# A two-layer attention and expert kernel: double-width products in every second u block, a joint pair choice, and another order of the v blocks

## The chip, the cores and the metric

The kernel runs on one core of a Trainium2 chip. The metric is device time in microseconds (us), from several executions of one program. TensorE (PE) does the matrix products and loads their stationary operand (PEld). VectorE (DVE), ScalarE (ACT) and GpSimd (POOL) work on tiles in on-chip memory, and SyncE (SP) starts most transfers. Each engine works through its own queue in order and waits on semaphores.

## The reference, cut to what matters

Two layers, each an attention mixer and an expert layer with residuals, on 256 tokens of width 1024. The change lies in the expert layer and in the step from layer 0's expert layer to layer 1's mixer (`fox`).

```python
def peer_ffn(x, w_q, sub_keys, u, v):        # 8 heads, 128x128 experts, 16 picked per head
    q = (x @ w_q).reshape(B, S, 8, 2, 128)
    s_half = jnp.einsum('bshpc,hpkc->bshpk', q, sub_keys)
    top_s, top_i = lax.top_k(s_half, 16)
    cand_s = top_s[..., 0, :, None] + top_s[..., 1, None, :]
    cand_i = top_i[..., 0, :, None] * 128 + top_i[..., 1, None, :]
    best_s, best_pos = lax.top_k(cand_s.reshape(B, S, 8, 256), 16)
    experts = jnp.take_along_axis(cand_i.reshape(...), best_pos, axis=-1)
    gate = jax.nn.softmax(best_s, axis=-1)
    h = jax.nn.gelu(einsum(u[experts], x))
    return einsum(gate * h, v[experts])
```

## The kernel before, in words

The kernel does not gather experts. For all 16384 experts, in 128 blocks of 128, it forms the products with u, applies gelu, multiplies by a gate that is zero where an expert is not picked, and multiplies by v. fp32 operands are kept as two parts, `hi` (rounded) and `lo` (the rest), and a product is three matrix products.

**The u sweep** is the loop over `b in range(NB)`, NB = 128, in `peer`. `load_split` (L727 and after) loads one block (512 KB) into `raw`, ACT casts it to `hi` (L116) and DVE subtracts to give `lo` (L117); each of the three tags has three buffers. `feat_block` runs, for each of 8 chunks, three products of 256 columns: hi with `xh` (L744), hi with `xl` (L747), lo with `xh` (L748). The result lies in a PSUM tile of the tag "h", which has two buffers. `values` applies gelu on ACT (L981, L984), and on DVE multiplies the tokens whose gates are already there (L985).

Beside it runs a list of small steps, `steps()`: the rest of `top_keys`; then `best_pairs`, which chooses 16 of 50 candidate pairs for each head and token and turns positions into expert numbers with masks (L881 to L930); then 32 `gate_steps` of 8 tokens, each with four DVE products of 1024 elements (L952 to L956), 16 TensorE products (L963, L964), and multiplications or copies into the gate store (L970, L972). Each step yields an estimated price, and after block b steps are taken until 1.66 us times b+1 are spent. This sets only the order in which instructions are written; a list scheduler then orders each engine's queue by its own cost model, with the written order as priority, and moves a later instruction forward where buffers and data allow. `pin` keeps an instruction in its written place.

**The gate store**: blocks 0 to 63 lie in `gte`, which takes the tile tagged "E" (one buffer); blocks 64 to 127 lie in `arena`, 256 columns each. The residual `h` lies in `arena` columns 10240 to 12287, the place of blocks 104 to 111, and waits in DRAM meanwhile (`h_out`, `h_in`).

**The v sweep** takes blocks 64 to 127, then `h_in`, then 0 to 63. `v_gate` splits the gates of two blocks (128x512), `v_whole` loads and splits a block of v with `load_split`, and 12 products of 512 columns accumulate in four PSUM tiles (L1020 to L1022). The last two blocks are held back for `fin(tt, nh)`, which finishes one accumulator and adds it to `h` (L1050).

**The step to layer 1**: after `fin`, `nxt.piece` transposes `h` (L150) for the next norm. `fox` takes the tile "E" anew as `HL`; `w_half` loads half of a weight tile into `arena` and splits it into `HL`. The first two halves are split with the subtraction on POOL (`(GP, GP)`), the next two with it on DVE.

Of the kernel before, what the change touches and what calls it, by code (L numbers as in the profile page):

```python
# [14 lines left out]
ALU = mybir.AluOpType  # L15
# [24 lines left out]
def body(ctx, tc, A, out):  # L40
# [4 lines left out]

    const = ctx.enter_context(tc.tile_pool(name="const", bufs=1))
    arena = const.tile([P, LC], F32, name="arena")
    xh = const.tile([P, 8, S], F32R, name="xh")
    xl = const.tile([P, 8, S], F32R, name="xl")
    cst = const.tile([P, 160], F32, name="cst")  # L50
    ident = cst[:, :P]
    gcols = cst[:, P:].rearrange("p (i c) -> p i c", i=4)
# [64 lines left out]
        (eng or V).tensor_tensor(lo, raw, hi.bitcast(F32), ALU.subtract)  # L117

    def squares(ss, tt, nh, junk):
        ACT.activation(ar(junk + nh * 512, 512), h[:, tt, nh * 512:nh * 512 + 512], AF.Square, accum_out=ss[:, nh:nh + 1])  # L120

    def rstd_of(ss, tt):

# [134 lines left out]
    def nsa():  # L258
# [329 lines left out]
        h_in(xsrc)  # L588
        return out_proj(HL, A["w_out0"], oh, ol, 1, [marks[i] for i in (2, 5, 7)]), marks[7]

    def fox(norm):
        HL = tl(big, "E", [16384], F32R, 1)
        oh = view(HL[:, 12288:14336], (8, S))
        ol = view(HL[:, 14336:16384], (8, S))
        qa = ar(6144, 16, S)
        ka = ar(10240, 16, S)
        vt = ar(14336, 2, D)
        wsrc = [A["w_in1"][:, off * 8:(off + n) * 8].rearrange("p (c n) -> p c n", c=8) for off, n in FOX_TILES]

        ws = [w_half(HL, wsrc[4][:, i * 4:i * 4 + 4], 512, (GP, GP)) for i in range(2)]  # L600
        for nh in range(2):
            steps = [lambda: norm.piece(1, 0), lambda: norm.piece(1, 1)]
            o = proj_tok(HL, wsrc[4 + nh], 512, xh, xl, ws=None if nh else ws, steps=steps)
# [147 lines left out]
    def peer(li, norm, mark):  # L751
# [97 lines left out]
        off += 512  # L849
        msk = [ar(off + i * 1024, 1024).bitcast(F16).rearrange("p (h j k) -> p h j k", h=8, j=16) for i in range(2)]  # L850
        off += 2048
        assert off <= LC - 2048, off

        hkT = tl(vst, "hkT", [4, S], F16, 1)
        def picked(m, x, dst):

            for q in range(2):
                hs = slice(4 * q, 4 * q + 4)
                V.tensor_tensor(m[:, hs], m[:, hs], x[:, hs].unsqueeze(3).broadcast_to((P, 4, 16, 16)), ALU.mult)
                yield 1.2  # L860
            for n in (8, 4, 2):
                V.tensor_tensor(m[:, :, :n], m[:, :, :n], m[:, :, n:2 * n], ALU.add)
            V.tensor_tensor(dst, m[:, :, 0], m[:, :, 1], ALU.add)
            yield 1.6

        def best_pairs():

            for tt in range(2):
                V.tensor_copy(idxh[:, tt], idx[:, tt].rearrange("p (h u) k -> p h u k", u=2))
                V.tensor_copy(dl[:, tt, :, 0:1], idxh[:, tt, :, 0, 0:1])  # L870
                V.tensor_tensor(dl[:, tt, :, 1:16], idxh[:, tt, :, 0, 1:16], idxh[:, tt, :, 0, 0:15], ALU.subtract)
                o_ = 0
                for a in range(9):
                    n = CAND_N[a] if a < 8 else 8
                    if a < 8:
                        i0 = top[:, tt, :, 1, 0:n]
                        i1 = top[:, tt, :, 0, a:a + 1].broadcast_to((P, 8, n))
                    else:
                        i0 = top[:, tt, :, 0, 8:16]
                        i1 = top[:, tt, :, 1, 0:1].broadcast_to((P, 8, n))  # L880
                    V.tensor_tensor(cand[:, tt, :, o_:o_ + n], i0, i1, ALU.add)  # L881
                    o_ += n
                    if a in (2, 8):
                        yield 1.0
                for hh in range(8):
                    c1 = cand[:, tt, hh]
                    c2 = cand2[:, hh % 2]
                    V.max(best[:, tt, hh, 0:8], c1)
                    V.max_index(pos[:, tt, hh, 0:8], best[:, tt, hh, 0:8], c1)
                    V.match_replace(c2, best[:, tt, hh, 0:8], c1, FMIN)  # L890
                    V.max(best[:, tt, hh, 8:16], c2)
                    V.max_index(pos[:, tt, hh, 8:16], best[:, tt, hh, 8:16], c2)
                    yield 1.25
                V.tensor_tensor(gf[:, tt], best[:, tt], best[:, tt, :, 0:1].broadcast_to((P, 8, 16)), ALU.subtract)

                V.tensor_copy(posh[:, tt], pos[:, tt])
                for hh in range(8):
                    V.tensor_tensor(msk[0][:, hh], posh[:, tt, hh].unsqueeze(1).broadcast_to((P, 16, 16)), st3, ALU.is_ge)
                    if hh % 4 == 3:
                        yield 1.3  # L900
                yield from picked(msk[0], dl[:, tt], i12[:, tt, 0])

                V.tensor_scalar(bh[:, tt], posh[:, tt], -42.0, 0.0, ALU.add, ALU.max)
                V.tensor_tensor(bh[:, tt], posh[:, tt], bh[:, tt], ALU.subtract)
                for i, (st, ln) in enumerate(((16, 16), (24, 8), (29, 5), (33, 4), (36, 3), (38, 2), (40, 2), (42, 2))):
                    V.tensor_scalar(th[:, tt], posh[:, tt], float(st), float(ln), ALU.is_ge, ALU.mult)
                    V.tensor_tensor(bh[:, tt], bh[:, tt], th[:, tt], ALU.subtract)
                    if i % 4 == 3:
                        yield 1.7
                for hh in range(8):  # L910
                    V.tensor_tensor(msk[1][:, hh], bh[:, tt, hh].unsqueeze(1).broadcast_to((P, 16, 16)), jt3, ALU.is_equal)
                    if hh % 4 == 3:
                        yield 1.15
                yield from picked(msk[1], idxh[:, tt, :, 1, :], i12[:, tt, 1])
                g3 = gf[:, tt]
                pin(ACT.activation(g3, g3, AF.Exp))
                gs = smt("gs", [8])
                V.tensor_reduce(gs, g3, AX.X, ALU.add)
                V.reciprocal(gs, gs)
                V.tensor_scalar(gs, gs, GSC, None, ALU.mult)  # L920
                V.tensor_tensor(g3, g3, gs.unsqueeze(2).broadcast_to((P, 8, 16)), ALU.mult)
                yield 4.2
# [8 lines left out]
                yield 0.3  # L931

# [11 lines left out]
        def gate_steps():  # L944


            for t0 in range(0, S, 8):
# [25 lines left out]
                    done[1] += 4  # L973
                yield 1.2

        def values(b, o):
            n = done[1]
            (x, _, _), = slots(b, b + 1, slice(0, S))
            x = x[:, 0]
            if n < S:  # L980
                ACT.activation(x[:, n:], o[:, n:S], AF.Gelu_apprx_tanh)  # L981
            if n > 0:
                gt = t2k(S)
                ACT.activation(gt[:, :n], o[:, :n], AF.Gelu_apprx_tanh)  # L984
                V.tensor_tensor(x[:, :n], gt[:, :n], x[:, :n], ALU.mult)  # L985
            done[0] = b + 1
# [5 lines left out]

        aux, spent = steps(), 0.0
        for b in range(NB):
            values(b, feat_block(load_split(uT[b])))
            if b < 2:
                scores(14 + b, qTs[14 + b])
            while spent < 1.66 * (b + 1):
                spent += next(aux, 1e9)

        acc = [[pst("m", bufs=4) for _ in range(2)] for _ in range(2)]
# [26 lines left out]
                for tt in range(2):  # L1028
                    v_mm(tt, nh, gg, vv[nh], first)

        for b in range(NE, NB):
            v_block(b, b == NE)
        h_in()
        if li == 1:
            gain = t4k(D)
            SP.dma_start(gain, A["final_norm"].broadcast_to((P, D)))
        for b in range(NE - 2):
            v_block(b)

        tail = []  # L1040
        for b in range(NE - 2, NE):
            gg = v_gate(b)
            tail.append((gg, v_whole(b)))

        def fin(tt, nh):
            for i, (gg, vv) in enumerate(tail):
                v_mm(tt, nh, gg, vv[nh], last=i == 1)
            for q in range(2):
                hs = slice(nh * 512 + q * 256, nh * 512 + q * 256 + 256)
                V.tensor_tensor(h[:, tt, hs], acc[tt][nh][:, q * 256:q * 256 + 256], h[:, tt, hs], ALU.add)  # L1050

        if li == 0:
            nxt = Norm(2, xh, xl, 6144)
            fin(0, 0)
            fin(0, 1)
            fin(1, 0)
            nxt.piece(0, 0)
            fin(1, 1)
            nxt.piece(0, 1)
# [97 lines left out]
```

## Time and profile before

| | |
|---|---|
| runs shown | 1953.0, 1954.05, 1956.66 us (median 1954.05) |
| the profiled execution | 1953.7 us, of which the span of its records is 1951.9 us |
| busy share of the span | PE 98%, PEld 88%, DVE 72%, ACT 51%, POOL 6% |
| layer 0 by time | mixer and query products to 242 us, u sweep to about 650 us, v sweep and `fin` to 1004 us |
| layer 1 by time | mixer from 1004 us, u sweep to about 1595 us, v sweep to 1943.7 us, end 1951.9 us |

Busy PE time counts each product from its start to its modelled end, and successive products overlap, so the pace of a stretch is read from start to start of the products.

### The profile page before, as it was taken

Reading aid. Unit: us, or ns where it says so; the run is one execution under the profiler, and the core shown is the slowest. Engines: PE = TensorE matmul, PEld = TensorE weight load, DVE = VectorE, ACT = ScalarE, POOL = GpSimd, SP = SyncE. Lnnn points to the kernel's source line nnn. Section 1 sums busy time; section 2 is a strip of 40 time slices with the busy share of each in tenths; the row PEclk is TensorE's granted clock in tenths of the full one; section 3 lists DMA queues with packets and bytes.
Section 4 is the critical chain, followed back from the end, with each engine's and each line's share of the span. In section 5 each row is a group of like instructions: output and inputs, shape, how many; then the busy total and the mean of one; then the engine's idle time right before and its main releaser. Section 6 shows DMA issues by size and latency. Waiting matters only on the chain.

```text
span 1951.9 us, 34088 instructions
## 1 busy us (share of the span) xinstructions
PE 1913.0 (98%) x13131; PEld 1718.6 (88%) x13131; DVE 1411.2 (72%) x3006; ACT 994.0 (51%) x1886; POOL 120.5 (6%) x80
## 2 busy tenths in 40 slices
PE   8889999999999999999999999999999999999998
PEld 6767999999999888888879799999999998888886
DVE  8687999478888655555586799956788975555555
ACT  5475645554444444444464655445544444444444
POOL 2001700000000000000040061000000000000001
PEclk9989999999999999999999999999999999999999
DMA  6623555554555666666654245565555556666664
GB/s 231 226 76 120 161 164 185 184 160 155 162 154 160 212 232 214 195 193 192 194 191 172 71 154 160 174 192 164 158 157 161 153 174 194 193 215 205 194 194 140
DMA packets 90194, 340.92 MB, mean 175 GB/s; under 512 B 9872, under 2 KB 12336, under 8 KB 84656
## 3 DMA queue, kind: packets, MB, share of 16 engines
q1 hardware_dynamic: 89744, 338.22, 54.6%
q8 instruction: 103, 1.69, 0.4%
q10 hardware_dynamic: 288, 0.52, 0.1%
q14 instruction: 59, 0.48, 0.1%
HBM read 334.48 MB, written 4.19 MB: 174 GB/s over the span
## 4 chain that ended last, share of the span: by engine, by line
PE 76%; DVE 15%; ACT 4%; issue 2%; DMA 1%; POOL 0%; SPq 0%; ACTq 0%; DVEq 0%
PE m L1021 12%; PE m L1022 12%; PE m L1020 12%; PE h L747 8%; PE h L744 8%; PE h L748 8%; DVE lo L117 5%; ACT hi L116 3%; PE m L963 2%; PE m L200 2%; PE m L202 2%; PE m L201 2%; PE m L964 1%; DVE vhl L956 1%; DVE vraw L955 1%
## 5 line engine op out<-in xcount | busy, mean ns | idle before, releaser
L117 DVE TENSOR_TENSOR lo<-raw,hi 128x1024 fp32r<-128x1024 f32 x516 | 634.9, 1231 | 397.9 <-ACT hi L116 394.3
L116 ACT CAST hi<-raw 128x1024 fp32r<-128x1024 f32 (+1 forms) x572 | 576.6, 1010 | 637.8 <-PE m L1022 294.7
L748 PE MATMUL h<-xh,lo 128*128 128x256 f32 x2048 | 581.5, 284 | 2.3 <-DVE lo L117 2.2
L744 PE MATMUL h<-xh,hi 128*128 128x256 f32 x2048 | 580.4, 283 | 1.4 <-ACT E L981 1.3
L747 PE MATMUL h<-xl,hi 128*128 128x256 f32 x2048 | 580.4, 283 | 0.0
L1021 PE MATMUL m<-lo,vhl 128*128 128x512 f32 x1024 | 399.0, 390 | 0.1
L1020 PE MATMUL m<-hi,vhl 128*128 128x512 f32 x1024 | 399.0, 390 | 0.0
L1022 PE MATMUL m<-hi,vhl 128*128 128x512 f32 x1024 | 398.8, 389 | 0.0
L748 PEld LDWEIGHTS h<-xh,lo 128*128 128x128 f32 x2048 | 386.6, 189 | 4.8 <-DVE lo L117 4.0
L744 PEld LDWEIGHTS h<-xh,hi 128*128 128x128 f32 x2048 | 386.4, 189 | 2.3 <-ACT E L981 2.0
L747 PEld LDWEIGHTS h<-xl,hi 128*128 128x128 f32 x2048 | 386.6, 189 | 0.0
L1021 PEld LDWEIGHTS m<-lo,vhl 128*128 128x128 f32 x1024 | 192.5, 188 | 40.4 <-DVE lo L117 0.5
L1020 PEld LDWEIGHTS m<-hi,vhl 128*128 128x128 f32 x1024 | 192.5, 188 | 40.1
L1022 PEld LDWEIGHTS m<-hi,vhl 128*128 128x128 f32 x1024 | 192.5, 188 | 39.7
L117 POOL TENSOR_TENSOR lo<-raw,hi 128x512 fp32r<-128x512 f32 x56 | 79.4, 1438 | 242.4 <-ACT hi L116 242.3
L972 ACT ACTIVATE arena<-m 128x256 f32<-128x256 f32 (+25 forms) x128 | 37.6, 303 | 79.9 <-DVE arena L970 75.9
L117 DVE TENSOR_TENSOR E<-arena,E 128x1024 fp32r<-128x1024 f32 (+2 forms) x60 | 70.8, 1208 | 10.1 <-ACT E L116 9.7
L744 PE MATMUL h<-E,hi 128*128 128x256 f32 x240 | 70.3, 293 | 3.0 <-ACT arena L817 3.0
L116 ACT CAST E<-arena 128x1024 fp32r<-128x1024 f32 (+2 forms) x68 | 62.2, 956 | 17.8 <-PE m L660 9.7
L117 DVE TENSOR_TENSOR vhl<-E,vhl 128x512 fp32r<-128x512 f32 x64 | 44.1, 688 | 34.1 <-ACT vhl L116 34.1
L748 PE MATMUL h<-E,lo 128*128 128x256 f32 x240 | 68.1, 284 | 0.0
L963 PE MATMUL m<-vhl 128*128 128x128 f16 x512 | 65.4, 218 | 2.7 <-DVE vhl L956 0.2
(300 smaller groups left out, 2476.9 us busy)
## 6 DMA issues: line engine op xcount, KB each, us to landing
raw<-in_u SPq DMA_DIRECT2D x256, 512.0 KB, 3.5
raw<-in_v SPq DMA_DIRECT2D x256, 512.0 KB, 4.2
arena<-in_w_in SPq DMA_DIRECT2D x18, 1024.0 KB, 5.2
raw<-in_wq SPq DMA_DIRECT2D x32, 512.0 KB, 3.7
arena<-in_w SPq DMA_DIRECT2D x8, 1024.0 KB, 5.3
arena<-in_w_out SPq DMA_DIRECT2D x8, 1024.0 KB, 5.1
hd<-arena SPq DMA_DIRECT2D x3, 1024.0 KB, 5.7
arena<-hd SPq DMA_DIRECT2D x3, 1024.0 KB, 5.9
```

The lines of the kernel that those rows point to most:

```text
L116: ACT.copy(hi, raw)
L117: (eng or V).tensor_tensor(lo, raw, hi.bitcast(F32), ALU.subtract)
L200: PE.matmul(o[:, :n], sh[:, cc, tsl], wh[:, c], start=cc == 0, stop=False)
L201: PE.matmul(o[:, :n], sh[:, cc, tsl], wl[:, c], start=False, stop=False)
L202: PE.matmul(o[:, :n], sl[:, cc, tsl], wh[:, c], start=False, stop=cc == 7)
L744: t = PE.matmul(o[:, :S], hi[:, c % 4], sh[:, c], start=c == 0, stop=False)
L747: PE.matmul(o[:, :S], hi[:, c % 4], sl[:, c], start=False, stop=False)
L748: PE.matmul(o[:, :S], lo[:, c % 4], sh[:, c], start=False, stop=c == 7)
L963: PE.matmul(o, o2[:, k, :, u], oh[:, k, :, u], start=True, stop=False)
L1020: PE.matmul(acc[tt][nh], gh[:, ts], vh, start=first, stop=False)
L1021: PE.matmul(acc[tt][nh], gh[:, ts], vl, start=False, stop=False)
L1022: PE.matmul(acc[tt][nh], gl[:, ts], vh, start=False, stop=last)
```

## The change

Four things. First, `xh` and `xl` become the two halves of one tile `x2`, so that `wide_block` can multiply `hi` with both in one product of 512 columns; odd u blocks use it: 8 products of 512 and 8 of 256 columns in place of 24 of 256. The two halves of the result are then added, with a copy on ACT and an addition on DVE. Second, `best_pairs` does both token halves in one instruction where it can, and `picked` writes its mask in one instruction and uses doubled tables (`d2`, `s2nd`); the budget falls from 1.66 to 1.5. Third, v goes 96 to 111, 0 to 63, 64 to 95, 112 to 127, `h_in` follows the first 16 blocks, three blocks are held back, and the norm's squares go to a small ring (`t2k`). Fourth, `fox_early` takes "E" in the last part of layer 0's v sweep and loads and splits `fox`'s first weights in eight pieces between v blocks, on ACT and DVE.

```diff
-    xh = const.tile([P, 8, S], F32R, name="xh")
-    xl = const.tile([P, 8, S], F32R, name="xl")
+    x2 = const.tile([P, 8, 2, S], F32R, name="x2")
+    xh, xl = x2[:, :, 0], x2[:, :, 1]
...
     def squares(ss, tt, nh, junk):
+        x = t2k(512) if junk is None else ar(junk + nh * 512, 512)
...
+    def fox_early():
+        HL = tl(big, "E", [16384], F32R, 1)
+        ring[0] = 2
+        raws = []
+        for i in range(2):
+            hi, lo = (view(HL[:, i * 4096 + x:i * 4096 + x + 2048], (4, 512)) for x in (0, 2048))
+            for q in range(4):
+                raw = t2k(1, 512)
+                SP.dma_start(raw, fox_src[4][:, i * 4 + q:i * 4 + q + 1])
+                split(raw, hi[:, q:q + 1], lo[:, q:q + 1])
+                yield
+            fox_ws.append((hi, lo))
+        fox_ws.append(HL)
...
     def fox(norm):
-        HL = tl(big, "E", [16384], F32R, 1)
+        ws, HL = fox_ws[:2], fox_ws[2]
...
-        ws = [w_half(HL, wsrc[4][:, i * 4:i * 4 + 4], 512, (GP, GP)) for i in range(2)]
...
-        def picked(m, x, dst):
-            for q in range(2):
-                hs = slice(4 * q, 4 * q + 4)
-                V.tensor_tensor(m[:, hs], m[:, hs], x[:, hs].unsqueeze(3).broadcast_to((P, 4, 16, 16)), ALU.mult)
-                yield 1.2
+        def picked(m, table, op, y, x2_, dst):
+            m2 = m.rearrange("p h j (k u) -> p (h j) k u", u=2)
+            V.tensor_tensor(m, y.unsqueeze(2).broadcast_to((P, 8, 16, 16)), table.unsqueeze(1).broadcast_to((P, 8, 16, 16)), op)
+            yield 1.2
+            V.tensor_tensor(m2, m2, x2_.rearrange("p h j u -> p (h j) u").unsqueeze(2).broadcast_to((P, P, 8, 2)), ALU.mult)
+            yield 1.2
...
         def best_pairs():
+            both = lambda x: x.rearrange("p t h k -> p (t h) k")
+            V.tensor_copy(d2, both(dl).unsqueeze(3).broadcast_to((P, 16, 16, 2)))
+            V.tensor_copy(s2nd, ih[:, :, 1, :].unsqueeze(3).broadcast_to((P, 16, 16, 2)))
...
-                for hh in range(8):
-                    V.tensor_tensor(msk[0][:, hh], posh[:, tt, hh].unsqueeze(1).broadcast_to((P, 16, 16)), st3, ALU.is_ge)
-                yield from picked(msk[0], dl[:, tt], i12[:, tt, 0])
...
+            pin(ACT.activation(g3, g3, AF.Exp))
+            for tt in range(2):
+                yield from picked(msk[0], st3, ALU.is_ge, posh[:, tt], d2[:, 8 * tt:8 * tt + 8], i12[:, tt, 0])
...
+        def wide_block(parts):
+            o = pst("h")
+            for c in range(8):
+                hi, lo = parts[c // 4]
+                PE.matmul(o, hi[:, c % 4], x2[:, c].rearrange("p a t -> p (a t)"), start=c == 0, stop=False)
+                PE.matmul(o[:, :S], lo[:, c % 4], xh[:, c], start=False, stop=c == 7)
+            u = t2k(S)
+            ACT.copy(u, o[:, S:])
+            V.tensor_tensor(u, o[:, :S], u, ALU.add)
+            return u
...
-            values(b, feat_block(load_split(uT[b])))
+            values(b, (wide_block if b % 2 else feat_block)(load_split(uT[b])))
...
-            while spent < 1.66 * (b + 1):
+            while spent < 1.5 * (b + 1):
...
-        for b in range(NE, NB):
-            v_block(b, b == NE)
-        h_in()
...
-        for b in range(NE - 2):
-            v_block(b)
+        order = list(range(NE + 32, NE + 48)) + list(range(NE)) + list(range(NE, NE + 32)) + list(range(NE + 48, NB))
+        early = fox_early() if li == 0 else iter(())
+        for i, b in enumerate(order[:-3]):
+            if i == 16:
+                h_in()
...
+            v_block(b, i == 0)
+            if i > 84 and i % 4 == 1:
+                next(early, None)
...
-        for b in range(NE - 2, NE):
+        for b in order[-3:]:
             gg = v_gate(b)
             tail.append((gg, v_whole(b)))
...
-            nxt = Norm(2, xh, xl, 6144)
+            nxt = Norm(2, xh, xl, None)
...
-                squares(ss, tt, nh, 6144)
+                squares(ss, tt, nh, None)
```

## Rows read from the trace of the kernel before

**Rows 1.** The page: busy us (share of span) xinstructions; granted clock by slice.

```profile
PE 1913.0 (98%) x13131; PEld 1718.6 (88%) x13131; DVE 1411.2 (72%) x3006; ACT 994.0 (51%) x1886; POOL 120.5 (6%) x80
PEclk9989999999999999999999999999999999999999
```

**Rows 2.** Windows: stretch, length, busy us of PE, PEld, DVE, ACT, POOL, PEclk.

```profile
243.00:339.00 96.00, 94.61 (x778) 92.94 (x778) 93.02 (x345) 47.98 (x75) 0.00 (x0) 1.00 0.55 175
395.00:640.00 245.00, 243.59 (x2253) 240.43 (x2252) 207.39 (x374) 119.12 (x292) 0.00 (x0) 1.00 0.51 160
550.00:600.00 50.00, 49.77 (x468) 49.11 (x467) 45.51 (x81) 23.34 (x57) 0.00 (x0) 1.00 0.51 162
645.00:990.00 345.00, 345.00 (x1545) 286.57 (x1544) 194.35 (x193) 168.94 (x195) 3.02 (x2) 1.00 0.66 206
985.00:1010.00 25.00, 21.50 (x93) 17.02 (x92) 20.41 (x40) 14.46 (x29) 15.61 (x5) 0.93 0.65 224
1230.00:1272.00 42.00, 39.76 (x318) 38.08 (x317) 40.80 (x122) 20.07 (x29) 0.00 (x0) 1.00 0.56 172
```

**Rows 3.** Timeline of PE in the u sweep: first and last of 52 consecutive products.

```profile
359.94 0.28 PE L744 MATMUL h<-xh,hi 128*128 128x256 f32 x1
...
365.99 0.28 PE L744 MATMUL h<-xh,hi 128*128 128x256 f32 x1
```

**Rows 4.** Timeline of PE in the v sweep: first and last of 33 consecutive products.

```profile
749.65 0.39 PE L1021 MATMUL m<-lo,vhl 128*128 128x512 f32 x1
...
756.90 0.39 PE L1020 MATMUL m<-hi,vhl 128*128 128x512 f32 x1
```

**Rows 5.** Groups of DVE by line and shape, 228 to 344 us: busy, mean ns.

```profile
L859 DVE TENSOR_TENSOR arena<-arena 128x1024 f16<-128x1024 f16 x8 | 9.5, 1218 | 0.0
L907 DVE TENSOR_TENSOR arena<-arena 128x128 f16<-128x128 f16 x16 | 3.5, 220 | 0.2
L898 DVE TENSOR_TENSOR arena<-arena 128x256 f16<-128x256 f16 x16 | 3.5, 283 | 0.0
L906 DVE TENSOR_SCALAR arena<-arena 128x128 f16<-128x128 f16 x16 | 3.0, 189 | 0.2
L953 DVE TENSOR_TENSOR vhl<-iota,hkT 128x1024 f16<-128x1024 f16 x3 | 2.0, 683 | 0.0
L862 DVE TENSOR_TENSOR arena<-arena 128x512 f16<-128x512 f16 x4 | 1.7, 419 | 0.0
```

**Rows 6.** The page's groups: the subtraction that gives lo, whole program.

```profile
L117 DVE TENSOR_TENSOR lo<-raw,hi 128x1024 fp32r<-128x1024 f32 x516 | 634.9, 1231 | 397.9 <-ACT hi L116 394.3
```

**Rows 7.** Groups by line, 350 to 634 us: a copy-like ACT instruction on 256 PSUM columns.

```profile
L981 ACT ACTIVATE E<-h 128x256 f32<-128x256 f32 (+6 forms) x29 | 10.6, 366 | 0.0
```

**Rows 8.** Timeline at the step to layer 1, all engines but PEld, cut.

```profile
989.45 10.02 POOL L117 TENSOR_TENSOR E<-arena,E 128x1024 fp32r<-128x1024 f32 x3
993.86 6.70 DVE L117 TENSOR_TENSOR E<-arena,E 128x1024 fp32r<-128x1024 f32 x2
997.11 0.39 PE L1022 MATMUL m<-hi,vhl 128*128 128x512 f32 x1
1000.48 2.07 DVE L1050 TENSOR_TENSOR arena<-m,arena 128x256 f32<-128x256 f32 x6
1000.94 1.11 PE L150 MATMUL g<-cst,arena 128*128 128x128 f32 x4 [3.45 <-DVE arena L1050]
1001.71 0.78 PE L1020 MATMUL m<-hi,vhl 128*128 128x512 f32 x1
1003.99 0.56 PE L1022 MATMUL m<-hi,vhl 128*128 128x512 f32 x1
1004.39 0.60 PE L150 MATMUL g<-cst,arena 128*128 128x128 f32 x4
```

**Rows 9.** Timeline near the end: a block's first product, its successors' split, an addition.

```profile
1929.91 0.39 PE L1020 MATMUL m<-hi,vhl 128*128 128x512 f32 x1
1930.11 1.05 ACT L116 CAST hi<-raw 128x1024 fp32r<-128x1024 f32 x1 [1.15 <-PE m L1022]
1931.19 1.22 DVE L117 TENSOR_TENSOR lo<-raw,hi 128x1024 fp32r<-128x1024 f32 x1 [0.98 <-ACT hi L116]
1942.35 0.42 DVE L1050 TENSOR_TENSOR arena<-m,arena 128x256 f32<-128x256 f32 x1 [0.60 <-PE m L1022]
```

More of the change, by code (lines that the diff above doesn't have):

```diff
@@ L119, in squares @@
     def squares(ss, tt, nh, junk):
-        ACT.activation(ar(junk + nh * 512, 512), h[:, tt, nh * 512:nh * 512 + 512], AF.Square, accum_out=ss[:, nh:nh + 1])
+        x = t2k(512) if junk is None else ar(junk + nh * 512, 512)
+        ACT.activation(x, h[:, tt, nh * 512:nh * 512 + 512], AF.Square, accum_out=ss[:, nh:nh + 1])
     def rstd_of(ss, tt):
@@ L589, in nsa @@
         return out_proj(HL, A["w_out0"], oh, ol, 1, [marks[i] for i in (2, 5, 7)]), marks[7]
+    fox_src = [A["w_in1"][:, off * 8:(off + n) * 8].rearrange("p (c n) -> p c n", c=8) for off, n in FOX_TILES]
+    fox_ws = []
+    def fox_early():
[11 more added lines that the diff above has]
+        fox_ws.append(HL)
     def fox(norm):
-        HL = tl(big, "E", [16384], F32R, 1)
+        ws, HL = fox_ws[:2], fox_ws[2]
         oh = view(HL[:, 12288:14336], (8, S))
@@ L597, in fox @@
         vt = ar(14336, 2, D)
-        wsrc = [A["w_in1"][:, off * 8:(off + n) * 8].rearrange("p (c n) -> p c n", c=8) for off, n in FOX_TILES]
-        ws = [w_half(HL, wsrc[4][:, i * 4:i * 4 + 4], 512, (GP, GP)) for i in range(2)]
+        wsrc = fox_src
         for nh in range(2):
@@ L851, in peer @@
         off += 2048
+        d2 = ar(off, 256).bitcast(F16).rearrange("p (h k u) -> p h k u", h=16, k=16)
+        off += 256
+        s2nd = ar(off, 256).bitcast(F16).rearrange("p (h k u) -> p h k u", h=16, k=16)
+        off += 256
         assert off <= LC - 2048, off
         hkT = tl(vst, "hkT", [4, S], F16, 1)
-        def picked(m, x, dst):
-            for q in range(2):
-                hs = slice(4 * q, 4 * q + 4)
-                V.tensor_tensor(m[:, hs], m[:, hs], x[:, hs].unsqueeze(3).broadcast_to((P, 4, 16, 16)), ALU.mult)
-                yield 1.2
+        def picked(m, table, op, y, x2_, dst):
[4 more added lines that the diff above has]
+            yield 1.2
             for n in (8, 4, 2):
@@ L863, in picked @@
             V.tensor_tensor(dst, m[:, :, 0], m[:, :, 1], ALU.add)
-            yield 1.6
+            yield 1.5
         def best_pairs():
-            for tt in range(2):
[L869 to L884, printed above, removed]
-                for hh in range(8):
[L886 to L897, printed above, removed]
-                    V.tensor_tensor(msk[0][:, hh], posh[:, tt, hh].unsqueeze(1).broadcast_to((P, 16, 16)), st3, ALU.is_ge)
-                    if hh % 4 == 3:
-                        yield 1.3
-                yield from picked(msk[0], dl[:, tt], i12[:, tt, 0])
[L903 to L922, printed above, removed]
@@ new lines, in best_pairs @@
+            both = lambda x: x.rearrange("p t h k -> p (t h) k")
+            V.tensor_copy(idxh, idx.rearrange("p t (h u) k -> p t h u k", u=2))
+            ih = idxh.rearrange("p t h u k -> p (t h) u k")
+            V.tensor_copy(both(dl)[:, :, 0:1], ih[:, :, 0, 0:1])
+            V.tensor_tensor(both(dl)[:, :, 1:16], ih[:, :, 0, 1:16], ih[:, :, 0, 0:15], ALU.subtract)
+            V.tensor_copy(d2, both(dl).unsqueeze(3).broadcast_to((P, 16, 16, 2)))
+            V.tensor_copy(s2nd, ih[:, :, 1, :].unsqueeze(3).broadcast_to((P, 16, 16, 2)))
@@ new lines, in best_pairs @@
+            yield 2.0
+            cd, tp = cand.rearrange("p t h n -> p (t h) n"), top.rearrange("p t h u k -> p (t h) u k")
+            o_ = 0
+            for a in range(9):
+                n = CAND_N[a] if a < 8 else 8
+                if a < 8:
+                    i0, i1 = tp[:, :, 1, 0:n], tp[:, :, 0, a:a + 1].broadcast_to((P, 16, n))
+                else:
+                    i0, i1 = tp[:, :, 0, 8:16], tp[:, :, 1, 0:1].broadcast_to((P, 16, n))
+                V.tensor_tensor(cd[:, :, o_:o_ + n], i0, i1, ALU.add)
+                o_ += n
+                if a in (2, 8):
+                    yield 1.0
@@ new lines, in best_pairs @@
+            bs, ps_ = both(best), both(pos)
+            for hh in range(16):
+                c1 = cd[:, hh]
+                c2 = cand2[:, hh % 2]
+                V.max(bs[:, hh, 0:8], c1)
+                V.max_index(ps_[:, hh, 0:8], bs[:, hh, 0:8], c1)
+                V.match_replace(c2, bs[:, hh, 0:8], c1, FMIN)
+                V.max(bs[:, hh, 8:16], c2)
+                V.max_index(ps_[:, hh, 8:16], bs[:, hh, 8:16], c2)
+                yield 1.0
+            g3, ph, bb, tt_ = both(gf), both(posh), both(bh), both(th)
@@ new lines, in best_pairs @@
+            V.tensor_tensor(g3, bs, bs[:, :, 0:1].broadcast_to((P, 16, 16)), ALU.subtract)
+            pin(ACT.activation(g3, g3, AF.Exp))
+            V.tensor_copy(ph, ps_)
+            for tt in range(2):
+                yield from picked(msk[0], st3, ALU.is_ge, posh[:, tt], d2[:, 8 * tt:8 * tt + 8], i12[:, tt, 0])
+            V.tensor_scalar(bb, ph, -42.0, 0.0, ALU.add, ALU.max)
+            V.tensor_tensor(bb, ph, bb, ALU.subtract)
+            for i, (st, ln) in enumerate(((16, 16), (24, 8), (29, 5), (33, 4), (36, 3), (38, 2), (40, 2), (42, 2))):
+                V.tensor_scalar(tt_, ph, float(st), float(ln), ALU.is_ge, ALU.mult)
+                V.tensor_tensor(bb, bb, tt_, ALU.subtract)
+                if i % 4 == 3:
+                    yield 1.6
@@ new lines, in best_pairs @@
+            gs = smt("gs", [16])
+            V.tensor_reduce(gs, g3, AX.X, ALU.add)
+            V.reciprocal(gs, gs)
+            V.tensor_scalar(gs, gs, GSC, None, ALU.mult)
+            V.tensor_tensor(g3, g3, gs.unsqueeze(2).broadcast_to((P, 16, 16)), ALU.mult)
+            yield 1.0
+            for tt in range(2):
+                yield from picked(msk[1], jt3, ALU.is_equal, bh[:, tt], s2nd[:, 8 * tt:8 * tt + 8], i12[:, tt, 1])
+            for tt in range(2):
+                yield 2.0
@@ L1029, in v_block @@
                     v_mm(tt, nh, gg, vv[nh], first)
-        for b in range(NE, NB):
-            v_block(b, b == NE)
-        h_in()
-        if li == 1:
-            gain = t4k(D)
-            SP.dma_start(gain, A["final_norm"].broadcast_to((P, D)))
-        for b in range(NE - 2):
-            v_block(b)
+        order = list(range(NE + 32, NE + 48)) + list(range(NE)) + list(range(NE, NE + 32)) + list(range(NE + 48, NB))
[3 more added lines that the diff above has]
+                h_in()
+            if i == 100 and li == 1:
+                gain = t4k(D)
+                SP.dma_start(gain, A["final_norm"].broadcast_to((P, D)))
+            v_block(b, i == 0)
+            if i > 84 and i % 4 == 1:
+                next(early, None)
         tail = []
-        for b in range(NE - 2, NE):
+        for b in order[-3:]:
             gg = v_gate(b)
@@ L1046, in fin @@
             for i, (gg, vv) in enumerate(tail):
-                v_mm(tt, nh, gg, vv[nh], last=i == 1)
+                v_mm(tt, nh, gg, vv[nh], last=i == 2)
             for q in range(2):
```

1 line of the change is left out of this document (removed).

## The prediction

> **What bounds the kernel now.** I read the page first: PE is busy 98% of the span at the full granted clock almost everywhere [rows 1]. A busy PE need not be a PE at its peak, so next come the windows, to see which stretches have PE waiting and which engine is full there [rows 2]. In the v sweep PE is busy all of 345 us, with DVE at 56%: PE alone sets that pace. In the u sweep there are two parts. From 243 to 339 us, where the pair choice runs, DVE is busy 93.0 of 96 us and PE loses 1.4; in layer 1 the like stretch loses 2.2 of 42. From 395 to 640 us, where the gate steps run, DVE is at 85% (91% in its densest 50 us) and PE loses 1.4 of 245. So PE sets the u sweep too, with DVE close behind. Only one place shows PE idle for long: the step to layer 1 [rows 8].
>
> Then the timeline, for the pace of products. In the u sweep 51 steps take 6.05 us: 118.6 ns per product of 256 columns [rows 3]. In the v sweep 32 steps take 7.25 us: 226.6 ns for 512 [rows 4]. Twice the columns do not cost twice the time: a line through both gives 108.0 ns per 256 columns and 10.6 ns per product. That difference is what the first edit can collect.
>
> **Wide products.** A narrow block takes 24 x 118.6 ns = 2.847 us. A wide one takes 8 x 226.6 + 8 x 118.6 ns = 2.762 us, if products of the two widths keep their paces when they alternate. No row has this alternation. From both sides: if two products joined save nothing, 512 columns cost 237.2 ns and the gain is nil; if the product of 256 gains because its neighbour's long run hides its weight load, it could fall to the line's 108.0 ns of columns, 0.085 us more for a block. I take the paces of the rows, which lie between: 0.085 us a block, 64 wide blocks a layer, two layers, **10.9 us**.
>
> A rule speaks against this. The Trainium skill, "TensorE: Matmul & The Clock Gate", section "Back-to-back issue gap", puts the warm gap at columns over 2.4 GHz plus about 2.5 ns. By it a wide block saves only 8 x 2.5 = 20 ns and the sweep term is an estimated 2.6 us in place of 10.9. This trace does not agree: it has 118.6 ns where the rule gives 109, and 226.6 where it gives 216.
>
> The wide block adds an ACT copy and a DVE addition. The nearest rows are an activation of 256 PSUM columns, 0.366 us [rows 7], and an addition of 256 columns from PSUM, 0.42 us [rows 9]. Per layer that is 23 us of ACT and 27 of DVE. ACT is half idle and pays nothing. The two PSUM buffers give block b its release deadline: b+2 needs it, and PE spends 2.8 us on b+1 meanwhile. Copy and addition need 0.79, so 2.0 us remain for queueing on DVE. Behind a late addition wait the gelu on ACT, then the cast of `hi` that stands behind it, then `lo`.
>
> **The pair choice.** It is DVE work inside the stretch where DVE is full. Each of four `picked` calls had eight masks of 283 ns and two products of 1218 ns, 4.70 us; it now has two instructions of 2048 elements. None is in the trace; from 419 ns for 512 and 683 for 1024 [rows 5] they come to 1.21 us each (1.37 at most, if twice the 1024). The doubled table matters here: the slow product repeats each value singly, while the gate steps' products of 683 ns repeat pairs. So 4.70 becomes 2.42, four times: 9.1 us less. The thresholds, 16 pairs of 189 and 220 ns (6.5 us), become 8 pairs of 256 elements at no more than 283 each (4.5): 2.0 less. Candidate sums and gate scaling halve their count: I put 1.5. The two doubled copies cost 0.4 each. Net DVE loses some 12 us a layer there, against 17 wide additions (7 us) in the same stretch. In the gate part 36 wide additions bring 15 us to 207 of 245, but 1.5 in place of 1.66 spreads the steps over a tenth more blocks, and a step's four products plus its multiplications are about 3.9 us, so some 11 us leave that stretch. DVE stays near 87%. I therefore book no gain, and **2.5 us of loss** over both layers for additions that come late now and then: the bound below is a gain of the waits seen (1.4 + 1.4 + 2.2 us, and 1.4 if layer 1's gate part is like layer 0's: some 6 us); the bound above is a rival.
>
> **The order of v and the early weights.** The step to layer 1 shows why PE idles. POOL splits the first weights for 12 us up to 999.5, DVE does two splits of the next in 6.70 us, where such an instruction has a mean of 1.231 [rows 6, 8], and the additions that `nxt.piece` needs (L1050) stand behind them until 1000.48. PE waits 3.45 us. Then its clock is at half: products start 0.456 us apart on average from 1001.71 to 1003.99, against 0.227, and four transposes take 1.11 us, later 0.60. That is 6 x 0.229 + 0.5 = 1.9 us, less what the window's mean clock leaves (25 us x 0.07 = 1.75 [rows 2]). I take 1.75. All POOL splits go, "E" is free some 45 blocks earlier, so the next two DVE splits can also move forward into a v sweep with DVE at 56%; if they do not, they cost 2 x 1.23 us with POOL silent, and PE has two more rounds of `fin` (9 products, 2.04 us each) to cover them. So **5.2 us** go; the lower end is 3.
>
> The eight early pieces bring 8 x (0.6 + 0.7) us to ACT and DVE and eight DMAs of 256 KB to SP, in 30 blocks (82 us) of a sweep where PE is never short: nothing. If that cover went, they would cost at most one DVE instruction each, 5 us.
>
> Holding back three blocks brings a wait. The third one's buffers come free when the block before the tail ends; after a block's first product at 1929.91, `lo` is ready at 1932.41, 2.5 us on [rows 9]. PE needs it after seven products of 226.6 ns, 1.59 us. So PE may wait 0.9 us in each layer, unless the scheduler puts another accumulator's products first: I take **1.0** for both (0 to 1.8). At the very end the longer `fin` takes the first half's norm out of the way of the last additions: **0.3** less (0 to 0.5).
>
> **The sum** starts at the profiled execution, 1953.7 us (its span is 1951.9; the median of the runs is 0.35 above it): 1953.7 - 10.9 + 2.5 - 5.2 + 1.0 - 0.3 = **1940.8, say 1941 us**. Its own range follows from the ends above: 1933 with DVE's waits gone and nothing in the tail, 1948 with a dearer alternation or a few late additions.
>
> **Rivals.**
> - *The wide product saves no time on PE* (512 columns beside 256 cost as much as the three narrow ones). For it: alternation is not in the trace, and a rule exists that puts nearly all time in columns. Against: two measured paces. Time: 1940.8 + 10.9 = 1952. By the rule named above it would be an estimated 1949. Chance 0.07.
> - *Slower: the addition holds PSUM.* If DVE runs a `lo` (1.23) and two gate products (1.37) before the addition, that is 2.6 us against 2.0 of room, and PE waits 0.6. At each of 64 gate steps that is 38 us: 1941 + 38 = 1979 at its worst, some 1962 if half of them and the pair-choice stretch suffer. It decides at a mean wait of 0.12 us for each of 128 wide blocks (15.2/128); below that the change is no slower. For it: DVE at 91 to 97% in stretches, in-order queues, an order made by a cost model. Against: PE loses only 1.4 of 245 us at that load. Chance 0.11.
> - *The step to layer 1 keeps most of its stall*, because the scheduler leaves the third and fourth splits before the additions: 1941 + 4 = 1945. It lies in the main range; chance 0.08.
> - *The relief of DVE pays*: the PE waits in the pair stretch vanish: 1941 - 6 = 1935. Chance 0.1, inside the range.
>
> The forecast itself, in its own range, has the rest, 0.64. The wider range of **1933 to 1953** takes in all but most of the slower rival (0.09) and some 0.05 below. Differences under 0.2%, 3.9 us, can hardly be told from none. Faster by more (under 1950.2): 0.82. Within: the first rival and the mild end of the second, 0.1. Slower: 0.08.
>
> **What would show it.** Products of a wide block should start 227 and 119 ns apart, the u sweep (242 to 650 us) should be about 5 us shorter in each layer. At the step to layer 1 no POOL split, no DVE split before L1050, a granted clock near 1, and PE idle under 1 us. In the tail, one PE wait for `lo` of up to 0.9 us. DVE in the gate part near 87%, in the pair stretch still full but shorter. Wrong would be: new PE waits on the release of the tag "h" or on L117 in the u sweep, a pace of 237 ns for 512 columns, or a PE wait inside the v sweep where the early pieces run.

## The result, and the profile after

The changed kernel takes 1940.43 us (median of 4 runs, 1940.23 to 1942.22) against 1954.13 before; the ratio is 0.993, 95% interval 0.9913 to 0.9947: a gain of 0.7%, clear of the noise. The forecast was 1941. The profiled execution took 1940.31 us, its span is 1938.5.

The page of the kernel after; the second row is the first product of each pair in a wide block, with TensorE's idle time before it and its releaser:

```profile
PE 1903.8 (98%) x12107; PEld 1664.0 (86%) x12107; DVE 1435.6 (74%) x3016; ACT 1032.8 (53%) x2040; POOL 108.4 (6%) x76
...
L1002 PE MATMUL h<-x,hi 128*128 128x512 f32 x1024 | 372.5, 400 | 5.5 <-DVE vraw L1006 5.1
```

The windows that answer to [rows 2] (length; busy us of PE, PEld, DVE, ACT, POOL; PEclk):

```profile
243.00:339.00 96.00, 92.89 (x644) 85.74 (x643) 85.67 (x291) 52.13 (x89) 0.00 (x0) 1.00 0.53 172
395.00:640.00 245.00, 244.96 (x1971) 228.64 (x1970) 215.29 (x400) 134.85 (x333) 0.00 (x0) 1.00 0.50 164
...
645.00:985.00 340.00, 340.00 (x1504) 281.69 (x1503) 197.98 (x199) 170.22 (x200) 3.52 (x1) 1.00 0.65 215
985.00:1002.00 17.00, 17.00 (x82) 13.64 (x81) 12.61 (x41) 7.36 (x22) 0.00 (x0) 1.00 0.41 154
```

DVE has 10 us of air in the pair stretch, where it had 3; yet PE is idle 3.1 us there, where it was idle 1.4. In the gate part PE is now busy all but 0.04 us. At the step to layer 1 it is never idle and the granted clock stays at 1.00.

The spans differ by 13.4 us. By stages, from first product to first product:

| stage | before | after | difference | in the sum |
|---|---|---|---|---|
| mixer of layer 0 | 242.14 | 242.47 | +0.3 | 0 |
| u sweep, layer 0 | 408.00 | 404.17 | -3.8 | -4.2 |
| v sweep, step and mixer of layer 1 | 536.44 | 531.08 | -5.4 | -4.7 |
| u sweep, layer 1 | 408.76 | 404.10 | -4.7 | -4.2 |
| v sweep, layer 1, to its last product | 347.94 | 348.19 | +0.3 | +0.5 |
| from there to the end | 8.62 | 8.49 | -0.1 | -0.3 |

The size fits in every stage. Whether the reasons do is another question: the u term was the net of two numbers, and the experiments take it apart. Their u sweeps are compared by this length, because the first stage, whose work no edit changes, varied by 4 us from one execution to another (last section).

### The profile page after: what moved, and what is told of

It is laid out like the page before. It is cut to its first block, busy times and chain, and to the rows that moved or that the text cites. A ratio compares the mean times of both kernels' runs of the same rounds, so it can differ in the third digit from the quotient of the medians.

```text
span 1938.5 us, 32161 instructions
## 1 busy us (share of the span) xinstructions
PE 1903.8 (98%) x12107; PEld 1664.0 (86%) x12107; DVE 1435.6 (74%) x3016; ACT 1032.8 (53%) x2040; POOL 108.4 (6%) x76
## 4 chain that ended last, share of the span: by engine, by line
PE 87%; DVE 8%; ACT 2%; issue 1%; DMA 1%; POOL 0%; SPq 0%; ACTq 0%; DVEq 0%
PE m L1054 12%; PE m L1053 12%; PE m L1055 12%; PE h L1002 11%; PE h L761 6%; PE h L764 6%; PE h L765 6%; PE h L1003 6%; DVE lo L117 2%; PE m L203 2%; PE m L201 2%; PE m L202 2%; PE m L985 2%; PE m L986 2%; ACT hi L116 1%
## 5 line engine op out<-in xcount | busy, mean ns | idle before, releaser
L1002 PE MATMUL h<-x,hi 128*128 128x512 f32 x1024 | 372.5, 400 | 5.5 <-DVE vraw L1006 5.1
L1003 PE MATMUL h<-x,lo 128*128 128x256 f32 x1024 | 291.6, 285 | 0.0
L761 PE MATMUL h<-x,hi 128*128 128x256 f32 x1024 | 289.4, 283 | 0.9 <-ACT E L1014 0.9
L765 PE MATMUL h<-x,lo 128*128 128x256 f32 x1024 | 289.8, 283 | 0.0
L764 PE MATMUL h<-x,hi 128*128 128x256 f32 x1024 | 289.7, 283 | 0.0
L1002 PEld LDWEIGHTS h<-x,hi 128*128 128x128 f32 x1024 | 192.3, 188 | 47.0 <-DVE vraw L1006 8.8
L761 PEld LDWEIGHTS h<-x,hi 128*128 128x128 f32 x1024 | 193.2, 189 | 6.6 <-ACT E L1014 1.4
L765 PEld LDWEIGHTS h<-x,lo 128*128 128x128 f32 x1024 | 192.9, 188 | 0.0
L764 PEld LDWEIGHTS h<-x,hi 128*128 128x128 f32 x1024 | 192.8, 188 | 0.0
L1003 PEld LDWEIGHTS h<-x,lo 128*128 128x128 f32 x1024 | 192.6, 188 | 0.0
```

The lines of the kernel that those rows point to most:

```text
L761: t = PE.matmul(o[:, :S], hi[:, c % 4], sh[:, c], start=c == 0, stop=False)
L764: PE.matmul(o[:, :S], hi[:, c % 4], sl[:, c], start=False, stop=False)
L765: PE.matmul(o[:, :S], lo[:, c % 4], sh[:, c], start=False, stop=c == 7)
L1002: PE.matmul(o, hi[:, c % 4], x2[:, c].rearrange("p a t -> p (a t)"), start=c == 0, stop=False)
L1003: PE.matmul(o[:, :S], lo[:, c % 4], xh[:, c], start=False, stop=c == 7)
```

## The experiments

Each was timed 4 or 5 times beside the kernel before, whose medians were 1953.7 to 1955.2. All are edits of the changed kernel.

**No wide blocks.**

```diff
-            values(b, (wide_block if b % 2 else feat_block)(load_split(uT[b])))
+            values(b, feat_block(load_split(uT[b])))
```

> The changed kernel (median 1940.4 us) with narrow products in every u block. Theory A, the sum as predicted: the wide products bring 10.9 us less 2.5 of late additions, so this run gives about 1949. Theory B, from the changed trace: alternating products of 512 start 231.7 ns apart and not 226.6, so a wide block saves 0.049 us (6.3 in all), and PE waits some 7.6 us for PSUM that the addition on VectorE frees late; the wide part is then worth nothing net and this run gives 1939 to 1943. The gate steps' entry (TensorE waits 0.18 us at each of 64 steps in the kernel before, 0.03 in the changed one) tells whose gain that is: if it stays small here it belongs to the pair choice and the pacing, if it comes back (plus 9 us) to the wide blocks.

Measured: 1947.35 us, ratio 0.9966. The u sweeps take 408.67 and 407.74 us, as before the change. So wide blocks are worth 8.1 us there, and the pair choice alone is worth nothing, although it leaves DVE busy 80.4 of 96 us in the pair stretch (93.0 in [rows 2]). The pair stretch of this run, as in [rows 2]:

```profile
243.00:339.00 96.00, 94.27 (x776) 92.81 (x775) 80.44 (x270) 47.59 (x73) 0.00 (x0) 1.00 0.58 174
```

The time is nearer to A's, but A's reasons do not hold: the gate steps' entry comes back, and the rows show B's dearer pace and its waits. First the pace, on PE of the kernel after, in a wide block:

```profile
355.10 0.40 PE L1002 MATMUL h<-x,hi 128*128 128x512 f32 x1
355.33 0.28 PE L1003 MATMUL h<-x,lo 128*128 128x256 f32 x1
...
356.86 0.39 PE L1002 MATMUL h<-x,hi 128*128 128x512 f32 x1
```

Five pairs take 1.76 us, 0.352 each, where [rows 3] and [rows 4] give 0.345. Between gate steps a wide block lasts 2.81 us (median of 45) and a narrow one 2.85: it saves 0.04 us and not 0.085.

Then the entry of a gate step: the last DVE product, the product before on PE, and the first gate product; two steps, the upper of the kernel before.

```profile
444.33 0.69 DVE L956 TENSOR_TENSOR vhl<-vhl,hkT 128x1024 f16<-128x1024 f16 x1
...
444.69 0.28 PE L744 MATMUL h<-xh,hi 128*128 128x256 f32 x1
...
445.07 0.22 PE L963 MATMUL m<-vhl 128*128 128x128 f16 x1
```

```profile
425.11 0.68 DVE L978 TENSOR_TENSOR vhl<-vhl,hkT 128x1024 f16<-128x1024 f16 x1
...
425.96 0.39 PE L1002 MATMUL h<-x,hi 128*128 128x512 f32 x1
426.19 0.23 PE L985 MATMUL m<-vhl 128*128 128x128 f16 x1
```

Before, the gate product starts 0.05 us behind the end of DVE's (445.02) and 0.38 behind its predecessor, which paces 0.119: a wait. It is so at 62 of 64 steps, 0.18 us each on average. The view of waits shows only 0.2 us of it, because a product's modelled end (0.28) lies beyond the next one's turn. After the change 36 of 64 steps follow a 512-column product, start a median 0.28 us after DVE is done, and cost no wait; the other 28 lose 1.9 us together. Why the scheduler's order comes out so beside wide blocks was not taken apart.

Third, the PSUM wait, in the pair stretch of the kernel after: copy, lo, addition, next block's first product.

```profile
268.45 0.36 ACT L1005 COPY vraw<-h 128x256 f32<-128x256 f32 x1
...
269.59 1.21 DVE L117 TENSOR_TENSOR lo<-raw,hi 128x1024 fp32r<-128x1024 f32 x1
270.71 0.42 DVE L1006 TENSOR_TENSOR vraw<-h,vraw 128x256 f32<-128x256 f32 x1
...
271.18 0.50 PE L1002 MATMUL h<-x,hi 128*128 128x512 f32 x1 [0.77 <-DVE vraw L1006]
```

The copy is done at 268.81. DVE works through pair-choice instructions and a lo first, and PE waits for the buffer. Seven such waits cost 3.8 us in each layer.

An account of every step between product starts in both u sweeps closes the 8.1 us: pace -4.0, gate entries -9.2, waits over 0.12 us +4.3, all else +0.7. Waits under 0.12 us count as pace here, so pace and waits shift a little with where that line is drawn; the entries do not.

**Products in groups.**

```diff
             for c in range(8):
-                hi, lo = parts[c // 4]
-                PE.matmul(o, hi[:, c % 4], x2[:, c]..., start=c == 0, stop=False)
-                PE.matmul(o[:, :S], lo[:, c % 4], xh[:, c], start=False, stop=c == 7)
+                PE.matmul(o, parts[c // 4][0][:, c % 4], x2[:, c]..., start=c == 0, stop=False)
+            for c in range(8):
+                PE.matmul(o[:, :S], parts[c // 4][1][:, c % 4], xh[:, c], start=False, stop=c == 7)
```

> The changed kernel with the eight products of 512 columns of a wide block first and the eight of 256 behind them. If the 5 ns by which 512-column products are dearer come from the alternation of widths, they go back to 226.7 ns in 56 of 64 starts per eight blocks: 8 x 5 ns x 128 = 5 us less, about 1935.5. If they come from something else that runs beside them (reads of the split, the gate steps), the pace stays at 231 and the time at 1940. The wait for PSUM in the pair stretch should stay as it is in either case.

Measured: 1936.18 us, ratio 0.9908, near the figure, but not for the reason. PE in this kernel:

```profile
410.16 2.03 PE L1001 MATMUL h<-x,hi 128*128 128x512 f32 x8
412.03 1.12 PE L1003 MATMUL h<-x,lo 128*128 128x256 f32 x8
412.98 0.28 PE L761 MATMUL h<-x,hi 128*128 128x256 f32 x1
```

Eight products of 512 columns take 1.87 us, 234 ns each: no faster than alternating ones, and the block is still 2.82. So alternation is not why they are dearer than v's 227; what is stays open. The sweeps (401.7 and 401.8 us) are 2.4 shorter each. Half of that is there by the fourth wide block, where the first wait for an addition is gone: `lo` and the addition of the second wide block come earlier in DVE's queue (the addition ends at 256.92 us, in the changed kernel at 258.48), and PE does not lose the 0.9 us that it lost there. `lo` is needed later in a grouped block, which may be why the scheduler's order changed; no run separates it, nor the other half.

**ScalarE frees PSUM.**

```diff
-            u = t2k(S)
-            ACT.copy(u, o[:, S:])
-            V.tensor_tensor(u, o[:, :S], u, ALU.add)
+            u = t2k(2 * S)
+            ACT.copy(u, o)
+            V.tensor_tensor(u[:, :S], u[:, :S], u[:, S:], ALU.add)
```

> The changed kernel with ScalarE copying all 512 columns of a wide block out of PSUM, and VectorE adding the halves from on-chip memory, so that PSUM is freed without VectorE. Theory: the seven waits of TensorE per layer on that addition in the pair stretch (3.8 us a layer by starts) vanish, and the time is 1940.4 - 7 = 1933 to 1934. Rival: VectorE is full there, the wait only moves to the subtraction that gives lo, and the time stays within 2 us of 1940.4.

Measured: 1936.76 us, ratio 0.9915; the sweeps (402.45, 402.47) are 1.7 shorter each, half of the theory. The view of waits, PE in 243 to 350 us:

```profile
PE h L761 <- ACT E L1014: 3.9, 4, 1.8
```

No wait for the addition is left, but a new one. The wide block's gelu on ACT waits for the addition; the next narrow block's gelu, which frees the other buffer, stands behind it. At the longest of these waits ACT stands idle 3.70 us until DVE's addition is done, starts the first gelu at 280.53 us and the second at 281.79, and PE goes on at 282.21.

**No early weights** (`fox_early` left out; `fox` takes "E" and splits with `(GP, GP)` as before).

> The changed kernel with the first weights of the next mixer split at the step, on POOL, as before; the new order of v, the three blocks held back and all else stay. Theory: the early splits are what removed the stall, so it comes back with 3.5 to 5.5 us: 1944 to 1946. Rival: the longer last rounds (27 products behind the first accumulator) and the earlier end of the tile E cover the splits anyway: 1940 to 1942.

Measured: 1946.83 us, ratio 0.9958. From v's first product to layer 1's u sweep it takes 535.51 us, 4.4 more. But the stall is not at the step, where PE is busy throughout (17.00 of 17 us from 995 on). With "E" free early, the scheduler moved POOL's splits into the v sweep:

```profile
907.58 2.00 ACT L116 CAST E<-arena 128x1024 fp32r<-128x1024 f32 x2 [3.28 <-DMA arena<-in_w_in]
908.71 5.74 POOL L117 TENSOR_TENSOR E<-arena,E 128x1024 fp32r<-128x1024 f32 x2 [19.57 <-ACT E L116]
910.57 1.63 DVE L117 TENSOR_TENSOR lo<-raw,hi 128x1024 fp32r<-128x1024 f32 x1 [5.00 <-ACT hi L116]
...
912.12 2.88 DVE L117 TENSOR_TENSOR vhl<-arena,vhl 128x512 fp32r<-128x512 f32 x1
...
914.92 2.35 DVE L117 TENSOR_TENSOR lo<-raw,hi 128x1024 fp32r<-128x1024 f32 x2
...
916.19 0.50 PE L1056 MATMUL m<-lo,vhl 128*128 128x512 f32 x1 [0.89 <-DVE lo L117]
...
917.19 0.68 DVE L117 TENSOR_TENSOR vhl<-arena,vhl 128x512 fp32r<-128x512 f32 x1
```

DVE's split of a gate pair takes 2.88 us beside POOL and 0.68 alone. `lo` comes late, PE waits. The Trainium skill, "SBUF — State Buffer", section "Who interferes with whom", says that a VectorE instruction with two SBUF inputs contends with a GpSimd one that reads SBUF; the row agrees: 2.88 is the length of one of the two POOL splits.

POOL alone is not what costs, though. Two POOL splits from 883.26 us on stretch a gate split to 2.90 us in the same way, and PE loses nothing there. Beside the later pair a transfer is late as well: ACT waits 3.28 us for a half of the weights before it can cast it, and DVE 5.00 us for ACT. Another PE wait (0.76 us at 922.91) has no POOL split beside it; ACT had waited 7.08 us for `raw`. From 895 to 950 us ACT waits 24.8 us for `raw`, in the changed kernel 3.2. So the trace shows late transfers beside POOL's splits; how much of the 4.4 us each is worth was not taken apart.

**Both mends of the wide block together** (grouped products and ScalarE's copy).

> Both mends of the wide block at once: the 512-column products first, and ScalarE copying both halves out of PSUM. By stages, the first took 4.9 us from the two u sweeps and the second 3.3. If the two are independent, the sweeps are 8 us shorter than in the changed kernel and the time is about 1932. If both draw on the same waits in the pair stretch, it stays near 1935. The stall behind gelu, which waits for VectorE's addition on ScalarE and keeps the next block's gelu behind it, should remain in both cases (4 us a layer).

Measured: 1937.58 us, ratio 0.9912; sweeps 401.9 and 402.1. The two do not add up: with grouped products ScalarE's copy brings nothing, and the gelu stall remains (3.5 us in layer 0).

**The old budget.**

```diff
-            while spent < 1.5 * (b + 1):
+            while spent < 1.66 * (b + 1):
```

> The changed kernel with the budget of 1.66 us a block in place of 1.5. With the old pair choice and the old budget the two u sweeps were 1.3 us shorter each than in the changed kernel, although VectorE did some 10 us more work. If that gain belongs to the pacing of the steps, it shows here too: 1937.5 to 1938.5. If it belongs to the pair choice itself (its order, its wide masks), this run stays at 1940 to 1941. A tighter pacing could also bring waits at the gate steps: 1942.

Measured: 1940.41 us, ratio 0.9932. The budget has no effect.

**The old pair choice and budget**, wide blocks kept.

> The changed kernel with the pair choice of before (one token half after the other, narrow masks) and its budget of 1.66; wide blocks, v order and early weights stay. With narrow blocks the new pair choice brought nothing in the u sweeps (408.7 and 407.7 us against 408.0 and 408.8 before). Theory: it pays only for the wide blocks' additions, 12 us of VectorE a layer against 7, so without it TensorE waits more in the pair stretch and the time is 1944 to 1950. Rival: TensorE's waits come from the order in VectorE's queue and not from its load, and the time stays at 1940 to 1942.

Measured: 1938.13 us, ratio 0.9917; sweeps 402.80 and 402.85, 1.3 shorter each, with DVE fuller:

```profile
243.00:339.00 96.00, 93.37 (x651) 86.52 (x650) 95.42 (x361) 53.17 (x90) 0.00 (x0) 1.00 0.55 173
```

DVE is busy 95.4 us of 96, 9.8 more, and PE 0.5 more. The theory falls: the relief does not pay for the additions. With the new choice the budget had no effect, so the choice's instructions or their order are the likely reason; which, stays open.

**Every block wide**, with both mends.

> Every u block wide, with both mends. TensorE alone would gain another 64 x 0.085 us a layer, some 11 us, to 1921. VectorE gets 64 more additions of about 0.4 us a layer, 26 us; in the gate part it would stand at some 96% of the time. If there is still room, 1921 to 1926; if VectorE now sets the pace of the u sweep, 1932 to 1945, with waits of TensorE on PSUM or on lo through the whole sweep.

Measured: 1930.38 us, ratio 0.9877; sweeps 398.42 and 398.44. It fits neither figure. The kernel with both mends and every second block wide (sweeps 401.9 and 402.1) differs from this one in the 64 narrow blocks of a layer alone, so these bring 3.6 us a layer; 0.04 us of pace a block gives 2.6 of them.

**The addition on POOL**, with both mends, every second block wide.

```diff
-            V.tensor_tensor(u[:, :S], u[:, :S], u[:, S:], ALU.add)
+            GP.tensor_tensor(u[:, :S], u[:, :S], u[:, S:], ALU.add)
```

> Both mends, every second block wide, and the addition of the two halves on POOL in place of VectorE. POOL is idle in the u sweep, and an addition of 512 elements takes it 1.44 us, so one of 256 some 0.75. Theory: the gelu no longer stands behind VectorE's queue, the 4 us a layer of waits in the pair stretch vanish, and the time is 1925 to 1929. Rival: while POOL runs, VectorE's instructions take longer (3.39 us in place of 1.23 at the step to layer 1 in the kernel before), so lo comes late and nothing is gained, or the sweep grows: 1932 to 1945.

Measured: 1987.14 us, ratio 1.0169, beyond the rival's figure; sweeps 427.9 and 427.8. DVE by line in 395 to 640 us (one gate product), then PE's waits in 243 to 640:

```profile
L977 DVE TENSOR_TENSOR vraw<-vhl,hkT 128x1024 f16<-128x1024 f16 x26 | 24.9, 956 | 0.0
```

```profile
PE m L985 <- DVE vhl L978: 18.6, 27, 1.6
```

This gate product takes 956 ns where it took 683 in the changed kernel, the last one of a step (L978) 832 where it took 686, and PE waits for the last one at 27 gate steps. So the rival named the right thing, VectorE slower beside POOL, but mis-sized it. Here the entry wait is long enough to be seen.

**Two v blocks held back.**

> The changed kernel with two v blocks held back in place of three. The additions behind the first accumulator were done at 990.8 us and the transposes that need them began at 993.0, so three blocks leave 2.2 us to spare; two blocks take 2.04 us less work in that stretch, so there is no wait, or one of 0.3 us. The products are the same in number. Theory: the third block brings nothing measurable, 1940 to 1941. Rival: without it the transposes wait and the next half's additions come late too: 1942 to 1943.

Measured: 1940.72 us, ratio 0.9935. The third block brings nothing.

**Every block wide, old pair choice and budget.**

> Every u block wide with both mends (1930.4 us with the new pair choice), and the pair choice and the budget of before. If the old pair choice is worth 2.5 us here too, 1928. If VectorE's 10 us more in the pair stretch, where it was at 92 of 96 us, now count, TensorE waits there and the time is 1933 to 1940.

Measured: 1930.37 us, ratio 0.9877. Nothing gained or lost against the new choice.

**Every block wide, PSUM freed as in the change**, products grouped.

> Every u block wide, 512-column products first, but PSUM freed as in the change: ScalarE copies one half, VectorE adds from PSUM. With every second block wide, ScalarE's copy of both halves brought nothing once the products were grouped (1937.6 against 1936.2). With every block wide each PSUM buffer waits for VectorE. If order in VectorE's queue matters, the pair stretch loses 3 to 8 us more than with ScalarE's copy: 1934 to 1938. If not, 1929 to 1931.

Measured: 1927.01 us (1926.14 to 1928.07), ratio 0.9864 with interval 0.9849 to 0.9879: the fastest here, faster than both kernels, and below either expectation. Its windows:

```profile
243.00:339.00 96.00, 94.09 (x527) 81.04 (x526) 91.55 (x306) 58.24 (x106) 0.00 (x0) 1.00 0.54 179
395.00:640.00 245.00, 244.79 (x1684) 213.26 (x1683) 227.68 (x441) 154.32 (x376) 0.00 (x0) 1.00 0.51 166
```

DVE stands at 93% of the gate part and PE loses 0.2 us of 245. PE's waits on the addition are short ones (0.6 at most from start to start). With ScalarE's copy of both halves and every block wide PE waits up to 0.9 us for that copy: one, at 279.42 us, stands in ACT's queue behind a gelu that has waited 2.15 us for DVE's addition, so PE waits for DVE all the same, by way of ACT. ACT also has 13 us less in the gate part than with that copy. How much each of the two is worth was not taken apart.

## Why the prediction was right, point by point

**The wide product's pace** was mis-sized. The step took 2.762 us for a wide block from [rows 3, 4]; it takes 2.81 against 2.85 for a narrow one, so the pace brings 5.1 us of the 10.9 at most, and 4.0 in the account. The row taken for 512 columns came from another sweep, and the same shape there is no proof of the same pace. The rival that wide products save nothing was wrong as well, and the 20 ns a block of the estimate set against the sum were too few.

**Late additions** were booked with 2.5 us. The mechanism was the one named as the slower rival (a lo and other DVE work ahead of the addition), at 3.8 us a layer in the pair stretch, partly in place of waits that were there without wide blocks: 4.3 net for both layers, with the other waits over 0.12 us. It came to half of its deciding point, 7.6 of 15.2 us (15.4 by the sum's own terms), because it struck 14 of 128 wide blocks; the 64 gate steps, where the rival saw its worst, lost nothing by it. The copy's price was taken from a row whose mean mixes several shapes; it came out right, at 0.36 us.

**What the sum lacked** is the wait at the gate steps, 11 us before. It does not show in the view of waits; it lay in the starts. Wide blocks remove 9 us of it. The pace fell 6.9 us short and the late additions cost 1.8 more than booked, so that the unseen gain makes up for two mis-sized terms. This is luck: the u term, 8.4 expected and 8.5 measured, is right as a number and only partly as a reason. One sign that the prediction itself lists as wrong did show: new PE waits on the release of the tag "h".

**The pair choice** was sized well (12 us of DVE a layer; 12.6 less in the pair stretch without wide blocks) and rightly booked at no gain. The rival that relief of DVE pays is refuted; with every second block wide the new choice is even 2.3 us dearer than the old one, with every block wide the two are level. DVE in the gate part stands at 88%, as expected (87); in the pair stretch it is not "still full" but at 89%, and PE waits more there, not less.

**The step to layer 1**: 5.2 less 0.5 for the tail, 5.4 measured. Without the early pieces 4.4 of it are lost, so the new order alone is worth 0.9. But the stall at the step goes with the new order alone too; what the early pieces save is a loss in the v sweep, where the run without them has late transfers and POOL's splits. The prediction was right that DVE's splits move forward (two of them start at 923.83 us); it did not see that without the pieces POOL's would too. The v sweep hid the pieces, with PE busy 340.00 of 340 us. **The tail's wait** of 0.9 us did not come, as the scheduler put other products first:

```profile
988.03 0.68 PE L1053 MATMUL m<-hi,vhl 128*128 128x512 f32 x2
988.56 0.40 PE L1054 MATMUL m<-lo,vhl 128*128 128x512 f32 x1
```

Two products with `hi` in a row, then those with `lo`. **The end** brought 0.1 of 0.3.

## What to carry to other kernels

Read PE's waits from product start to product start: a wait shorter than the modelled overlap shows in no view of idle time, and 64 of 0.18 us were worth more than the pace. Freeing the second busiest engine brought nothing here, because the order in its queue decided what came late: DVE had 10 us of air where PE waited longest. POOL is not free help: beside one of its splits a VectorE instruction of 0.68 us took 2.88. And a stage that comes out at its forecast is no proof of the reasons; take its terms apart one by one.

## What the runs showed that was not expected

The same shape of product, 512 columns of fp32r, starts every 227 ns in the v sweep and, as a median, every 232 to 233 in the u sweep; grouping or alternating makes no difference to that. The reason stays open. And the mixer of layer 0, whose work no edit changes, ended between 241.5 and 245.8 us. Windows of one quick and one late execution (no wide blocks; no early weights):

```profile
60.00:110.00 50.00, 43.96 (x412) 35.93 (x409) 31.35 (x71) 31.27 (x75) 0.96 (x1) 1.00 0.70 235
```

```profile
60.00:110.00 50.00, 45.29 (x405) 36.90 (x404) 28.64 (x62) 29.16 (x67) 0.96 (x1) 0.93 0.67 227
```

The granted clock there is 1.00 in one and 0.93 in the other, that is, part of the stretch at 1.2 GHz. In the late one it fell at 60 us, after 5 us in which PE was busy for 2.15; the quick one was busy for the same 2.15 and kept 2.4 GHz, so what decides is not shown. Of all fourteen traces, the four whose mixer ended after 244 us are those with 0.91 to 0.93 in this window; the ten with 0.97 to 1.00 ended by 243.5. A difference of 3 us between two totals of this kernel can come from there, so stage lengths are the safer measure.
